# Counted places for the level runs, and float16 pairs for layer 1's mixer, in a two-layer hybrid attention block

## The chip, the cores and the metric

One NeuronCore of a Trainium2 chip runs the whole program. The metric is the device time of one execution in microseconds. The kernel is written by hand against the engines: TensorE (PE, with its weight loads as PEld), VectorE (DVE), ScalarE (ACT), GpSimd (POOL), and SyncE (SP), which issues nearly all DMAs. A scheduler places the instructions of each engine in one fixed order when the program is built; on the chip each engine then works through its own list in that order.

## The reference

512 tokens, 1024 features, two layers, all float32. Each layer is `x += mixer(rmsnorm(x))` and then `x += swiglu(rmsnorm(x))`; a last rmsnorm follows.

```python
def hybrid_mixer(h, ...):
    (hq, hf, hi, hog, gq, gk, gv, glr, gog, nq_, nkc, ..., ngate, mgate) = split_cols(h @ w_in)
    o_hg = chunked_gated_linear_attention(silu(hq), -expm1(log_f), hi, log_f)      # HGRN, 4 heads of 128
    y_hg = head_rmsnorm(o_hg, ...) * silu(hog)
    o_gla = chunked_gated_linear_attention(gq * 64 ** -0.5, gk, gv, log_a)         # GLA, 4 heads of 64/128
    y_gla = head_rmsnorm(o_gla, ...) * silu(gog)
    y_nsa = nsa_attention(q, kc, vc, ks, vs, kw, vw, gates)                        # 8 heads of 64
    g = sigmoid(mgate).reshape(B, T, 3, 1024)
    m = g[:, :, 0] * (y_hg @ w_br_hg) + g[:, :, 1] * (y_gla @ w_br_gla) + g[:, :, 2] * (y_nsa @ w_br_nsa)
    return m @ w_out

def swiglu(h, w_gate, w_up, w_down):                                               # 1024 -> 2816 -> 1024
    return (silu(h @ w_gate) * (h @ w_up)) @ w_down
```

## The kernel before, in words

**Dense products.** All weights are read once, in pieces of 128 x 1024 float32 (512 KB). A product is exact to float32 by pairs: both operands are split into a high and a low part, and `mm3` (L267) issues three matmuls of 128x128 by 128x512 for each block: high by high, high by low, low by high. `mm3` also chains every dense block after the one before (`dense_last`), so the dense matmuls of the program have one fixed order, 3600 a layer; other matmuls may be placed between them.

Two kinds of pairs exist. In the mixers, `wout`, FFN-down and the first two FFN pieces the parts are float32r: `weights` (L165) loads a piece into `wraw` (two buffers, DMA issued by SP), ACT copies it to `whi` (L282), and DVE subtracts to `wlo` (L283). In the rest of the FFN's gate and up the parts are float16: `scaled` (L186) loads into `xg` (eight buffers), ACT takes the sum of squares (`squares`, L184), POOL sums it over the partitions, DVE makes a power of two from it (`power`), and `split_by` scales and splits (L207, L208). The moving side of those is made by `x16` (L218), which also takes the norm's factor `rb` in, so the result needs one scale `ginv` at eviction and not `rb`.

**The mixer's dense work.** Column pieces (`A`: `hq`, `hf`, `gk`, `gq`, `hog`, `gog`, `mgate`, 44 of them) have the features on the partitions and are evicted by `evac` on DVE (L534: PSUM times `rb`). Token pieces (`Bg`: `hi`, `gv`, `n1`, `n2`, four pieces each, and the three uneven pieces of `w3` in `small`) go through `dense_t` with the tokens on the partitions. The products of the branches (`wbr`) and `wout` follow. `fill` spreads the 24 `mgate` pieces and the branch products over the later heads and over NSA, where they stand between the attention's small matmuls. `norm` makes `xg` (float32r pairs of x times the gain) and `rb`, and the factors per token (`rs`) with eight one-column matmuls (L348).

**Heads and level runs.** `attend` (L399) does one HGRN head, or two GLA heads at a time: 12 calls in all, six a layer. Its intra-chunk scores are made in seven levels. For each level `gated` takes ACT (L430) and DVE (L431, L434, L436) one after the other, from the level before; the results lie in `ahl`, which has four buffers. After each second level (and after the seventh) PE does a *level run*: 24 small float16 matmuls (12 for the last; twice as many for two GLA heads) into a PSUM buffer `s` (three of them), from which DVE copies by mask (L458). So an `attend` has four level runs, the program 48. The third and fourth need `ahl` buffers that the first frees. After them come the state products (L473), the output `o` (L492) and `finish`. Where a level run stands among the dense matmuls was the scheduler's choice.

**Order around layer 0's FFN.** After 22 pairs of gate and up (`for f`, L727), FFN-down has eight output blocks of 66 matmuls (L743), then layer 1 begins with `norm`, `hq` and `hf` of head 0, of head 1, and `hi`.

## Time and profile before

| | |
|---|---|
| median of 3 runs | 1904.47 us (1903.38 to 1906.08) |
| profiled execution, its own time | 1905.07 us |
| its span, first to last instruction | 1903.3 us |
| mean granted TensorE clock | 0.998 |
| layer 0: mixer and `wout` / FFN | to about 600 / to about 955 us |
| layer 1: mixer and `wout` / FFN | to about 1539 / to the end |

Times in rows are microseconds from the span's start. A busy time of PE counts modelled ends: a 128x512 matmul is shown as some 0.38 to 0.40 us long while the next one starts after less than 0.23, so a stream of them shows PE as busy throughout, and the pace is read from the starts. "Idle before" counts only what lies past the modelled end of the instruction before.

### The profile page before, as it was taken

To read this page: it belongs to the slowest core of one execution; us is meant where nothing else is said; L and a number is where in the kernel's file an instruction comes from. 1 tells how busy PE (TensorE), PEld (TensorE's weight loads), DVE (VectorE), ACT (ScalarE), POOL (GpSimd) and SP (SyncE) were. 2 spreads that over 40 slices of the span, in tenths; PEclk is the share of its full clock that TensorE was granted. 3 is DMA by queue.
4 is the path that set the end of the run, shared out by engine and by line. 5 is a ranking of instruction groups with operands and counts; after the bars stand their busy time and mean duration, and the time that the engine had idled before them with its cause. 6 is when DMAs were issued, how large, how long until landed. Compare 5 with 4: busy or idle time off the path is not lost.

```text
span 1903.3 us, 27551 instructions
## 1 busy us (share of the span) xinstructions
PE 1872.6 (98%) x10642; PEld 1359.3 (71%) x10642; DVE 1186.4 (62%) x2242; ACT 1020.6 (54%) x1766; POOL 43.2 (2%) x100
## 2 busy tenths in 40 slices
PE   9999999999999999999999999999999999999998
PEld 7778777777788444468887787777778874444787
DVE  7677867689766534323367787767896774443233
ACT  6556655378745755322255566543886466553222
POOL 0000000000000000000000000000000000000000
PEclk9999999999999999999999999999999999999999
DMA  4222213248733533023332222132586344330222
GB/s 164 84 72 77 78 62 100 78 95 162 193 100 95 207 100 103 30 71 107 116 95 78 75 74 81 53 106 73 118 168 164 116 155 144 101 110 1 89 89 97
DMA packets 142467, 194.24 MB, mean 102 GB/s; under 512 B 91552, under 2 KB 94208, under 8 KB 142336
## 3 DMA queue, kind: packets, MB, share of 16 engines
q1 hardware_dynamic: 142048, 192.35, 34.6%
q8 instruction: 83, 1.36, 0.3%
q14 instruction: 48, 0.39, 0.1%
q10 hardware_dynamic: 288, 0.14, 0.0%
HBM read 167.29 MB, written 4.19 MB: 90 GB/s over the span
## 4 chain that ended last, share of the span: by engine, by line
PE 80%; DVE 9%; issue 6%; ACT 3%; DMA 1%; POOL 0%; DVEq 0%; SPq 0%; ACTq 0%; POOLq 0%
PE mmf L271 8%; PE mmf L270 8%; PE mmf L269 8%; PE mm L269 5%; PE mm L271 5%; PE mm L270 5%; PE mmmgate L269 4%; PE mmmgate L271 4%; PE mmmgate L270 4%; PE s L998 2%; DVE wlo L283 2%; PE o L492 2%; DVE at L458 2%; DVE ahl L431 1%; PE o L1047 1%
## 5 line engine op out<-in xcount | busy, mean ns | idle before, releaser
L282 ACT ACTIVATE whi<-wraw 128x1024 fp32r<-128x1024 f32 (+2 forms) x242 | 232.5, 961 | 334.0 <-PE mm L270 122.5
L283 DVE TENSOR_TENSOR wlo<-wraw,whi 128x1024 fp32r<-128x1024 f32 (+2 forms) x242 | 266.4, 1101 | 163.5 <-ACT whi L282 158.7
L269 PE MATMUL mmmgate<-xg,whi 128*128 128x512 f32 x384 | 153.4, 399 | 0.0
L271 PE MATMUL mmmgate<-xg,wlo 128*128 128x512 f32 x384 | 151.5, 395 | 0.2
L270 PE MATMUL mmmgate<-xg,whi 128*128 128x512 f32 x384 | 151.3, 394 | 0.0
L208 DVE SCALAR_TENSOR_TENSOR whi<-xg,gsc,whi 128x1024 f16<-128x1024 f32 x38 | 48.8, 1284 | 138.0 <-ACT whi L207 138.0
L430 ACT ACTIVATE ahl<-kq 128x512 f16<-128x512 f32 x84 | 55.1, 656 | 79.1 <-DVE kq L434 66.2
L184 ACT ACTIVATE v<-xg 128x1024 bf16<-128x1024 f32 x76 | 79.9, 1051 | 26.8 <-DMA xg<-w 26.1
L207 ACT ACTIVATE wlo<-xg,gsc 128x1024 f16<-128x1024 f32 x38 | 43.6, 1147 | 78.2 <-PE mmf L271 78.2
L271 PEld LDWEIGHTS mmmgate<-xg,wlo 128*128 128x128 f32 x384 | 72.2, 188 | 15.3 <-DVE wlo L283 1.1
L269 PEld LDWEIGHTS mmmgate<-xg,whi 128*128 128x128 f32 x384 | 72.3, 188 | 14.3
L270 PEld LDWEIGHTS mmmgate<-xg,whi 128*128 128x128 f32 x384 | 72.3, 188 | 12.9
L739 DVE SCALAR_TENSOR_TENSOR ld<-mmf,ginv,ld 128x512 f32<-128x512 f32 x40 | 30.0, 750 | 73.5 <-PE mmf L271 73.5
L130 ACT ACTIVATE ld<-s,nm 128x128 f32<-128x128 f32 (+3 forms) x128 | 65.8, 517 | 15.4 <-DVE nm L1017 12.1
L271 PE MATMUL mmn<-whi,xg 128*128 128x512 f32 (+1 forms) x192 | 70.4, 367 | 0.0
L269 PE MATMUL mmn<-whi,xg 128*128 128x512 f32 (+1 forms) x192 | 70.2, 366 | 0.0
L1027 DVE SCALAR_TENSOR_TENSOR ahl<-ld,sums,ahl 128x128 f16<-128x128 f32 (+3 forms) x128 | 65.7, 547 | 6.7 <-ACT ahl L1026 5.9
L270 PE MATMUL mmn<-wlo,xg 128*128 128x512 f32 (+1 forms) x192 | 69.6, 362 | 0.0
L1026 ACT ACTIVATE ahl<-ld,sums 128x128 f16<-128x128 f32 (+3 forms) x128 | 65.2, 552 | 4.5 <-DVE sums L1023 1.8
L130 ACT ACTIVATE ld<-mmf,ginv 128x512 f32<-128x512 f32 x40 | 27.4, 684 | 73.8 <-PE mmf L271 73.8
L431 DVE TENSOR_TENSOR ahl<-kq,ahl 128x512 f16<-128x512 f32 x84 | 59.0, 702 | 7.1 <-ACT ahl L430 7.0
L1017 DVE TENSOR_REDUCE nm<-s 128x1 f32<-128x384 f32 (+3 forms) x96 | 56.3, 592 | 5.6 <-PE s L998 5.2
(474 smaller groups left out, 4982.7 us busy)
## 6 DMA issues: line engine op xcount, KB each, us to landing
wraw<-w SPq DMA_DIRECT2D x188, 512.0 KB, 3.5
xg<-w SPq DMA_DIRECT2D x76, 512.0 KB, 3.5
wraw<-w SPq DMA_DIRECT2D x57, 256.0 KB, 2.6
xt<-xT SPq DMA_DIRECT2D x16, 256.0 KB, 5.8
lr<-cw SPq DMA_DIRECT2D x16, 256.0 KB, 5.8
xd<-xt SPq DMA_DIRECT2D x8, 256.0 KB, 3.1
xt<-xd SPq DMA_DIRECT2D x8, 256.0 KB, 5.6
wraw<-w SPq DMA_DIRECT2D x4, 444.0 KB, 3.2
```

The costliest lines, as they stand in the source:

```text
L130: i = self.nc.scalar.activation(out, in_, func, **kw)
L184: self.nc.scalar.activation(self.st("v1", list(x.shape), BF), x, AF.Square, scale=scale, accum_out=ss)
L269: first = mm(out, a[0], b[0], start=start, stop=False)
L270: mm(out, a[0], b[1], start=False, stop=False)
L271: last = mm(out, a[1], b[0], start=False, stop=stop)
L282: nc.scalar.activation(hi, x, AF.Copy)
L283: nc.vector.tensor_tensor(lo, x, hi.bitcast(F32), op=ALU.subtract)
L430: nc.scalar.activation(hi, kq, AF.Copy)
L431: nc.vector.tensor_tensor(lo, kq, hi, op=ALU.subtract)
L1017: nc.vector.tensor_reduce(nm, pv, axis=AX.XY, op=ALU.max, negate=True)
L1026: nc.scalar.activation(ahl[:, 0, b], a[:, b], AF.Copy, scale=sums[:, b:b + 1])
L1027: nc.vector.scalar_tensor_tensor(ahl[:, 1, b], a[:, b], sums[:, b:b + 1], ahl[:, 0, b], op0=ALU.mult, op1=ALU.subtract)
```

## The change

**Level runs.** Each level run's first matmul is noted in `runs`, and each `mm3` notes its three matmuls in `passes`. At the end of the build an order is added for those of the 48 with a number in `LEVELS_AT`: the run comes after that many dense matmuls. It waits for no semaphore; it fixes the order on PE. In the program before, the runs of layer 0 stood after (in the order of the list, 0 marking the same free ones) 216, 216, 234, 240; 384, 384, 405, 411; 552, 552, 581, 590; 720, 720, 751, 761; 912, 912, 929, 930; 1056, 1056, 1075, 1094 dense matmuls, and those of layer 1 within a few of the same plus 3600.

**Layer 1 in float16 pairs.** All of layer 1's `A` and `Bg` pieces and `w3`, but for `hq` and `hf` of heads 0 and 1, are split to float16 by a scale (`pieces16`), with the moving side from `x16`, held in eight `y` buffers; one piece lies in one `whi` or `wlo` buffer in turn, and not in one of each. The sums of squares come from `presums`: 59 further loads of these pieces into `xg` during layer 0's FFN, each with an ACT Square, one or two after each gate/up pair from the fourth on (28), then up to five after each FFN-down block (31). Layer 1 then loads the pieces again as before.

**With it.** `evac16` on DVE multiplies by the piece's scale in place of `rb`; for `mgate` it also clamps, so `gate`'s own clamp (L767) falls away in layer 1. Layer 1's per-token factors fall away. The gates `m` of layer 1's first branch lie in `xg`.

```diff
+LEVELS_AT = (0, 0, 240, 246, 0, 0, 414, 420, 0, 0, 588, 597, 726, 726, 756, 768, 0, 921, 942, 948, 0, 1068, 1086, 1104, 0, 0, 3843, 3849, 0, 0, 4020, 4026, 0, 0, 4194, 4206, 0, 4347, 4374, 4380, 0, 4521, 4545, 4551, 0, 4668, 4689, 4710)
...
+    def presums(self, l):
+        nc, io = self.nc, self.io
+        w = lambda n, i: (io["w"][l, PIECES[n] + i], D)
+        ones = [(n, i) for n in ("hq", "hf") for i in range(2, 4)]
+        ones += [(n, i) for n, c in A_TILES[2:] for i in range(c)]
+        fours = ("hi", "gv", "n1", "n2")
+        srcs = [w(*k) for k in ones] + [w(n, i) for n in fours for i in range(4)]
+        srcs += [(io["w3"][l, :, a:b], b - a) for a, b in CUTS3]
+        self.pre = {k: i for i, k in enumerate(ones + list(fours) + ["w3"])}
+        sums = self.st("misc", [P, len(srcs)])
+        for j, (src, n) in enumerate(srcs):
+            raw = self.st("xg", [P, n])
+            nc.sync.dma_start(raw, src)
+            self.squares(sums[:, j:j + 1], raw)
+            if j < len(srcs) - 1:
+                yield
...
+        self.pexp, self.pscale = self.power(g, "misc", "pexp", "pscale")
+
+    def pieces16(self, key, srcs):
+        at = self.pre[key]
+        out = []
+        with self.hp():
+            for src, n in srcs:
+                raw = self.st("wraw", [P, n])
+                self.nc.sync.dma_start(raw, src)
+                self.turn = 1 - self.turn
+                t = self.st(("whi", "wlo")[self.turn], [P, 2, n], F16)
+                self.split_by(t[:, 0], t[:, 1], raw, self.pscale[:, at:at + 1])
+                out.append((t[:, 0], t[:, 1], self.pinv[:, at:at + 1]))
+        return out
...
@@ mm3
         self.dense_last = last.ins
+        self.passes += [first.ins, None, last.ins]
...
@@ attend
                             if last is not None:
                                 self.after(ins, last)
+                            elif m == j == 0 and ps is pss[0]:
+                                self.runs.append(ins)
...
+    def evac16(self, tag, ps, inv, scale, floor):
+        t = self.st(tag, [P, T]) if isinstance(tag, str) else tag
+        with self.hp():
+            if scale is not None:
+                self.nc.vector.tensor_scalar(t, ps, inv, scale, op0=ALU.mult, op1=ALU.mult)
+            elif floor is not None:
+                self.nc.vector.tensor_scalar(t, ps, inv, floor, op0=ALU.mult, op1=ALU.max)
+            else:
+                self.nc.vector.tensor_scalar(t, ps, inv, None, op0=ALU.mult)
+        return t
...
@@ layer
-        xg, rb, rs = self.norm(x, sp["g1"], True, l == 0)
+        xg, rb, rs = self.norm(x, sp["g1"], not self.pre, l == 0)
+        if self.pre:
+            xh = self.x16(x, sp["g1"], rb, [self.st("y", [P, 2, T], F16) for _ in range(KD)])
+            self.pinv = self.st("pinv", [P, len(self.pre)])
+            nc.vector.tensor_scalar(self.pinv.bitcast(I32), self.pexp, self.xoff, None, op0=ALU.add)
...
+        def A(name, n, tag, scale=None, floor=None):
+            if (name, n) in self.pre:
+                w = self.pieces16((name, n), [(io["w"][l, PIECES[name] + n], D)])
+                ps, = self.pair16(w, xh, f"{name}{n}")
+                return self.evac16(tag, ps, w[0][2], scale, floor)
...
+        def T3(name, srcs, width):
+            if name in self.pre:
+                w = self.pieces16(name, srcs)
+                return self.dense_t(w, xh, width, name), [w[0][2]] * NT
...
+        more = self.presums(l + 1) if l + 1 < DEPTH else iter(())
         acts = self.act_slots()
         for f in range(NF):
...
             self.split(*acts[f], t1)
+            for _ in range(int(1.5 * f) - int(1.5 * (f - 1)) if f >= 3 else 0):
+                next(more, None)
         s = Stream(self, l, PIECES["down"])
         last = l == DEPTH - 1
         for n in range(KD - last):
...
+            for _ in range(5):
+                next(more, None)
...
     def mgate(self, A, br, d, tag):
-        g = A("mgate", br * KD + d, tag)
+        g = A("mgate", br * KD + d, tag, floor=-44.0)
         with self.hp():
-            self.gate(g)
+            self.gate(g, floor=False)
         return g
...
@@ build
+        for run, at in zip(k.runs, LEVELS_AT):
+            if at:
+                k.after(run, k.passes[at - 1].name)
```

## Rows read from the trace of the kernel before

**Rows 1.** The page's busy time: engine, us, share of the span, instructions.

```profile
PE 1872.6 (98%) x10642; PEld 1359.3 (71%) x10642; DVE 1186.4 (62%) x2242; ACT 1020.6 (54%) x1766; POOL 43.2 (2%) x100
```

**Rows 2.** Stretches: length; busy (count) PE, PEld, DVE, ACT, POOL; clock; DMA; GB/s.

```profile
958.00:1003.00 45.00, 44.96 (x198) 36.83 (x198) 27.29 (x42) 23.59 (x39) 1.69 (x2) 1.00 0.30 91
1003.00:1340.00 337.00, 327.98 (x2124) 260.69 (x2123) 255.88 (x514) 178.64 (x300) 9.36 (x21) 1.00 0.24 77
1340.00:1447.00 107.00, 106.52 (x847) 84.88 (x846) 96.37 (x253) 94.42 (x242) 0.00 (x0) 1.00 0.77 151
615.00:650.00 35.00, 34.55 (x160) 17.75 (x159) 22.64 (x43) 30.91 (x51) 3.67 (x7) 1.00 0.70 252
650.00:740.00 90.00, 90.00 (x419) 40.79 (x418) 38.93 (x63) 50.11 (x71) 3.58 (x9) 1.00 0.32 100
850.00:940.00 90.00, 90.00 (x390) 73.06 (x389) 31.59 (x34) 24.25 (x28) 0.00 (x0) 1.00 0.34 112
```

**Rows 3.** PE in time order, layer 1 `gv`: start, length, line, tiles, shape.

```profile
1069.94 0.40 PE L269 MATMUL mmgv<-whi,xg 128*128 128x512 f32 x1
...
1081.99 0.39 PE L271 MATMUL mmgv<-whi,xg 128*128 128x512 f32 x1
```

**Rows 4.** PE in time order, layer 0's FFN, float16.

```profile
700.02 0.38 PE L270 MATMUL mmf<-ahl,wlo 128*128 128x512 f16 x1
...
707.79 0.38 PE L270 MATMUL mmf<-lr,whi 128*128 128x512 f16 x1
```

**Rows 5.** Groups by line, the level runs: busy us, mean ns, idle before, releaser.

```profile
L452 PE MATMUL s<-ahl 128*128 128x64 f16 x672 | 24.1, 193 | 6.2 <-DVE ahl L431 6.2
L452 PE MATMUL s<-ahl 64*128 64x64 f16 x672 | 15.1, 190 | 9.3 <-DVE at L458 6.5 <-DVE ahl L431 2.8
```

**Rows 6.** Who waited for whom: us in total, times, longest.

```profile
PE s L452 <- DVE ahl L431: 9.0, 17, 1.1
```

**Rows 7.** PE in time order, layer 0, HGRN head 0, later level runs.

```profile
64.94 0.39 PE L271 MATMUL mmn<-whi,xg 128*128 128x512 f32 x1
65.95 0.86 PE L452 MATMUL s<-ahl 128*128 128x64 f16 x24 [0.61 <-DVE ahl L431]
...
68.13 0.51 PE L452 MATMUL s<-ahl 128*128 128x64 f16 x12
```

**Rows 8.** PE in time order, layer 0, GLA pair 0, first level runs.

```profile
247.30 1.24 PE L452 MATMUL s<-ahl 64*128 64x64 f16 x60
...
251.52 0.88 PE L452 MATMUL s<-ahl 64*128 64x64 f16 x36 [1.39 <-DVE at L458]
```

**Rows 9.** Layer 1 NSA stretch, instructions on tile `mmmgate` alone: PE, PEld, DVE.

```profile
1340.00:1447.00 107.00, 57.28 (x218) 39.46 (x216) 6.38 (x10) 1.00 0.77 151
```

**Rows 10.** Groups by line on DVE, columns as in 5.

```profile
L283 DVE TENSOR_TENSOR wlo<-wraw,whi 128x1024 fp32r<-128x1024 f32 x184 | 224.8, 1222 | 140.8 <-ACT whi L282 140.0 <-DMA lr<-cw 0.3
L208 DVE SCALAR_TENSOR_TENSOR whi<-xg,gsc,whi 128x1024 f16<-128x1024 f32 x38 | 48.8, 1284 | 138.0 <-ACT whi L207 138.0
L534 DVE TENSOR_TENSOR y<-mmmgate,rb 128x512 f32<-128x512 f32 x32 | 22.1, 690 | 41.0 <-PE mmmgate L271 40.9
L666 DVE TENSOR_SCALAR ld<-s,sp 128x512 f32<-128x512 f32 x4 | 3.0, 751 | 9.1 <-PE s L664 9.1
L767 DVE TENSOR_SCALAR y<-y 128x512 f32<-128x512 f32 x32 | 13.5, 421 | 0.3
```

**Rows 11.** Groups by line on ACT.

```profile
L282 ACT ACTIVATE whi<-wraw 128x1024 fp32r<-128x1024 f32 x184 | 194.7, 1058 | 283.1 <-PE mm L270 122.5 <-issue 58.2 <-PE mmmgate L270 37.0
L184 ACT ACTIVATE v<-xg 128x1024 bf16<-128x1024 f32 x76 | 79.9, 1051 | 26.8 <-DMA xg<-w 26.1
L207 ACT ACTIVATE whi<-xg,gsc 128x1024 f16<-128x1024 f32 x38 | 43.2, 1136 | 0.5 <-DVE gsc L180 0.5
```

**Rows 12.** PE in time order, layer 1's first norm.

```profile
956.23 0.95 PE L348 MATMUL s<-ones,og 128*128 128x1 f32 x8
```

**Rows 13.** The page's DMA issues: count, KB each, median us from issue to landing.

```profile
xg<-w SPq DMA_DIRECT2D x76, 512.0 KB, 3.5
```

89 lines of the change are left out of this document (54 added, 35 removed).

## The prediction

> **What bounds the kernel now.** I read the page's busy times first. TensorE is busy 98% of the span [rows 1], its granted clock 1.00 in every stretch I use [rows 2], so a microsecond counts only if it leaves TensorE's stream. The table of stretches says where it has company: in layer 1's heads DVE is busy 256 of 337 us, in its NSA stretch 96 of 107 with ACT at 94, while in the FFN's gate and up (650 to 740) and down (850 to 940) PE has no idle time at all and DVE is at 43% and 35% [rows 2]. A busy time with modelled ends hides the pace, so third I read PE's starts in order of time: 53 steps of float32r take 12.05 us, 227.4 ns each [rows 3]; 36 steps of float16 with the same 512 columns take 7.77 us, 215.8 ns [rows 4]. Fourth, what makes PE stand still: of the 1903.3 us of span PE is idle in 31 [rows 1], and the groups by line put 6.2 and 9.3 of these ahead of the level runs [rows 5]. The waits name the makers: 17 times the DVE subtraction that makes `ahl` [rows 6], and, in GLA, the mask copies that give back the PSUM buffer [rows 5, 8].
>
> So there are two removable things: some 20 us of standing still, half in each layer, and 11.6 ns in every converted matmul.
>
> **Part 1, the level runs.** An example: the matmul ahead starts at 64.94, the run at 65.95 [rows 7]. A dense neighbour would have started 0.23 us later, so 0.78 us are lost, of which the row shows 0.61 as idle; 0.16 us (0.39 us of modelled length less 0.23) is hidden in each such stall. With 17 stalls on `ahl` [rows 6] and 4 on the PSUM buffer (one in each GLA call; the program has two calls a layer), the total is 15.5 [rows 5] + 21 x 0.16 = 18.9 us.
>
> The new places take this away where the delay covers the chain. In HGRN head 0 the third run goes from 234 to 240 dense matmuls: 6 x 0.227 = 1.36 us against 0.78, and the fourth again 6 behind: 0.69 + 1.36 = 2.05 us after the third, against 2.18 before [rows 7], with 0.58 us in hand. Of the others that stalled, most are put 5 to 18 matmuls later, 1.1 us and more, so they are covered as well. In layer 1 six float16 matmuls are 1.29 us, and the same head's places (27 matmuls after the first runs, where layer 0 has 24) make up for that.
>
> GLA's second run is another case. Its later part waits for the mask copies and starts at 251.52; the first run starts at 247.30 and takes 0.7 us [rows 8]. Put 9 dense matmuls on, it comes at 248.0 + 2.05 = 250.1 and still meets copies that DVE does not reach earlier; its first 12 matmuls (60 less 48 in the row) need none of them and take 0.3. I leave 1.1 us in each of the four: -4.4. Part 1: 18.9 - 4.4 = **14.5 us** (bounds: 18.9 if DVE's order shifts in its favour; 0 if each delay comes out again behind the run). For the second bound: queued behind a late run on PE are the state products and `o` of its head, on DVE its mask copies. A head's turn is 168 dense matmuls (the places 216 to 384), 38 us, which for most of that time need none of this head's results, so 1.4 us later is not late. I take the upper half for that reason. Nothing else moves: the order waits for no semaphore, and no DMA and no other queue belongs to it.
>
> **Part 2, float16 in layer 1's mixer.** Converted are 40 column pieces of 24 matmuls and 16 token pieces of 24: 960 + 384 = 1344, each 227.4 - 215.8 = 11.6 ns shorter [rows 3, 4]: 15.6 us. The 96 of 296 columns in `w3` are not in the rows at float16; between nothing and the same saving in proportion, 96 x 6.7 ns = 0.6 us, I take 0.6. In NSA, 218 of the matmuls [rows 9] stand between attention steps where DVE is 90% busy and ACT 88% [rows 2]. If these set the pace there, 218 x 11.6 ns = 2.5 us don't arrive; I take off a third, 0.8. Part 2: **15.4 us** (bounds 13.1 to 17, the upper one with the contended steps at 0.229 us in place of 0.227).
>
> Both paces hold across stages: 90 us of gate and up hold 419 matmuls, 90 us of FFN-down in float32r 390 [rows 2]. The Trainium skill, "TensorE: Matmul & The Clock Gate", section "Back-to-back issue gap", gives the spacing as columns over 2.4 GHz plus 2.5 ns, 215.8 ns for 512, and names no data type there. The float16 rows agree to the digit; by that rule alone the conversion would be worth nothing, but the trace has 227.4 for float32r.
>
> What part 2 costs beside it:
> - DVE. Splitting a piece takes 1284 ns in place of 1222, ACT's half 1136 in place of 1058 [rows 10, 11]: 56 pieces, 3.5 and 4.4 us. An eviction that multiplies by a column from a per-partition scalar takes 751 ns (L666, also out of PSUM) against 690 [rows 10]: 40 x 0.06 = +2.4. Each `mgate` loses its clamp: 24 x 0.42 = -10.1. `x16` adds 8 x (0.75 + 0.69) = 11.5 us on DVE and some 5 on ACT. In the heads DVE goes from 256 of 337 to some 254 of 320, which hides it; in NSA it falls with PE. I cost it at nothing.
> - The added wait. The first float16 piece, `hi`, waits for `rb` and `x16`, and behind it stands the whole dense chain. Ahead of it are 96 float32r matmuls, 21.8 us, and its four pieces want two of the eight parts every 5.2 us. DVE has 27.3 of 45 us busy there [rows 2]; 11.5 more make 38.8. It fits; if DVE took the head's own chain first, the wait would cost some 5 us. The level chain of head 0 also comes later, but its first runs stand 120 matmuls behind `hi`'s start.
> - The per-token factors: eight matmuls of 0.95 us together drop out of PE's stream [rows 12]: **-0.8 us**.
>
> **Part 3, the sums of squares.** 59 loads of 512 KB on SP, 59 Squares of 1.05 us and an accumulator read on ACT, one POOL sum. In gate and up, ACT is busy 50.1 of 90 us [rows 2]; 1.5 Squares per pair of 10.4 us add 18%. The eight `xg` buffers then serve 3.5 loads a pair and still hold two pairs. In FFN-down, ACT is busy 24 of 90 us; up to five per block of 66 x 0.231 = 15.2 us add 41%. The DMA goes there from 112 GB/s to as much as 112 + 5 x 0.524 MB / 15.2 us = 284. The fastest stretch shown has 252 GB/s at a DMA share of 0.70, and PE lost 0.45 us of 35 in it [rows 2]. Cost: I take **+1.0 us**, twice that row, with 0 and 7 as ends (one late piece of 1 us at each of seven blocks; a gain is excluded, since nothing leaves this stage). The cover is the two raw and two split buffers of a stream that wants a piece every 24 x 0.23 = 5.6 us; what happens without it is the last rival.
>
> **The sum.** 1905.1 (profiled) - 14.5 - 15.4 - 0.8 + 1.0 = 1875.4. The median of the runs lies 0.6 under the profiled execution: **1875**, 1.5% faster.
>
> **The rivals.**
> - Stalls that move. The level runs come later, and so do their mask copies, state products and `o`; if PE then waits at those for what it no longer waits before, part 1 is worth nothing: 1905.1 - 15.4 - 0.8 + 1.0 - 0.6 = 1889. For it: the third run starts just when DVE lets it [rows 7], so this chain is a serial one, ACT to DVE to ACT. Against it: it is serial over 24 to 36 of a head's 168 dense matmuls.
> - The mixer's pace is DVE's and ACT's. Then part 2 gives nothing: 1890. For it: 90% in NSA [rows 2]; against it: 76% in the heads [rows 2], where most of the converted matmuls are.
> - One pace for both types: if the 11.6 ns belong to the busy mixer around the matmul and not to its type, they stay, and part 2 gives nothing: 1890 again. Against it: FFN-down is float32r and quiet, and still holds 390 where gate and up hold 419 [rows 2]. The Trainium skill's page named above has a rule that would come out here, one gap whatever the type.
> - Everything arrives: GLA's PSUM wait goes too, the contended steps count, and DVE's relief by the clamps shortens other chains: 1905.1 - 18.9 - 17 - 0.8 - 0.6 = 1868, with a few us more for the last point: 1862 to 1868.
> - Slower: sums of squares ahead of the weights. SP issues in order and the eight free `xg` buffers let it issue up to eight loads ahead of FFN-down's next piece. At 252 GB/s a load takes 2.1 us, so the piece lands 8 x 2.1 + 3.5 [rows 13] = 20 us after its issue. Two raw and two split buffers cover about 2 x 5.6 - 2.3 (splitting) = 9 us. PE would stand 11 us at each of seven blocks, +77 us: 1950. With five loads ahead it is 14 us against 9, +35 us: 1909. It decides from about five loads in a row, and an ACT that meets a Square whose load has not landed adds to it, since the next weights' split queues behind. Against it: nothing forces the loads to come in bursts, since each waits for a buffer that a Square gives back; and at 0.70 DMA share the trace shows no such stall. Milder forms end between 1885 and 1905.
> The Trainium skill, "DMA: Bandwidth & Descriptors", section "Queues, rings and completion order", says that on each DMA engine the descriptors of a ring are consumed in order; no row here shows two such loads overtaking or not, and by it the burst would cost what this rival says.
>
> **How the numbers follow.** Chances: forecast (1868 to 1883) 0.58; moved stalls 0.14; DVE's pace 0.07; one gap 0.02; everything arrives 0.11; sums of squares ahead of the weights 0.08, of which 0.06 end slower and 0.02 about level. About 0.2% is what a measurement of this kernel can tell from no change. Faster 0.92, same 0.02, slower 0.06. The range 1861 to 1891 takes in the bounds of all three parts and the cases about 1890; outside lie the slow rival and the last of the best case. Likeliest sign and likeliest time agree, so one range does.
>
> **What would show it.** Right: idle time ahead of L452 falls from 15.5 us to some 4, all of it in the GLA form; starts of `hog`, `gv` and `mgate` in layer 1 are 0.216 us apart; layer 1's mixer and `wout` are shorter by some 23 us, layer 0's mixer by some 7, and layer 0's FFN is as long as before. Wrong: idle time at L473, L492 or L998 that was not there (moved stalls); DVE over 95% in a stretch of layer 1 with PE waiting for `wlo`, `whi` or `s` (its pace); gaps in PE at FFN-down's first matmul of a piece, with ACT's split waiting for a DMA (loads ahead); a gap at the first `hi` matmul (`x16`).

## The result, and the profile after

The changed kernel takes **1891.9 us** (median of 6 runs, 1891.0 to 1892.9) against 1905.8 (median of 6 of the kernel before): a ratio of 0.993 [0.9917, 0.9943]. It is 13.9 us faster, where 30 were forecast, and lies just above the range. The profiled execution took 1891.8 us, 1890.0 of them span.

The busy times of the page, beside [rows 1]: TensorE has 17 us less, and is still at 98%; ACT has 67 us more.

```profile
PE 1855.3 (98%) x10634; PEld 1234.1 (65%) x10634; DVE 1193.3 (63%) x2244; ACT 1088.0 (58%) x1892; POOL 47.0 (2%) x102
```

**The pace came.** Layer 1's `gv` in order of time (start, length, line, tiles, shape), to be set beside [rows 3]:

```profile
1063.60 0.38 PE L309 MATMUL mmgv<-wlo,y 128*128 128x512 f16 x1
...
1069.42 0.38 PE L309 MATMUL mmgv<-whi,y 128*128 128x512 f16 x1
```

27 steps in 5.82 us are 215.6 ns each, where float32r had 227.4. The Trainium skill, "TensorE: Matmul & The Clock Gate", section "Back-to-back issue gap", has a formula that gives 215.8 ns for 512 columns and names no data type. The float16 rows agree, the float32r rows differ, and the measurement decides.

**The sums of squares cost nothing.** Stretches of layer 0's FFN (columns as in [rows 2]). The first two lines are gate and up and FFN-down of the kernel after; the third and fourth are the stretch with the most loads, after and before.

```profile
646.00:736.00 90.00, 90.00 (x419) 40.79 (x418) 38.56 (x63) 69.66 (x110) 4.41 (x11) 1.00 0.61 199
846.00:936.00 90.00, 90.00 (x391) 73.05 (x390) 31.23 (x34) 24.25 (x28) 0.00 (x0) 1.00 0.35 111
790.00:846.00 56.00, 56.00 (x255) 32.72 (x253) 19.85 (x32) 45.85 (x79) 1.15 (x3) 1.00 0.75 271
```
```profile
794.00:850.00 56.00, 56.00 (x255) 32.83 (x254) 18.50 (x22) 16.88 (x22) 0.00 (x0) 1.00 0.15 45
```

With 271 GB/s in place of 45, and ACT busy 46 of 56 us in place of 17, TensorE starts the same 255 matmuls in 56 us.

**The level runs are better, the state products worse.** Groups by line and shape (L491 is L452 of before, L514 is L473), then TensorE's waits (us, times, longest):

```profile
L491 PE MATMUL s<-ahl 128*128 128x64 f16 x672 | 24.0, 193 | 3.1 <-DVE ahl L470 3.1
L491 PE MATMUL s<-ahl 64*128 64x64 f16 x672 | 14.0, 190 | 7.6 <-DVE at L499 6.1 <-DVE ahl L470 1.5
L514 PE MATMUL s<-kq 128*128 128x256 f32 x32 | 10.1, 399 | 5.9 <-DVE kq L483 4.3 <-DVE kq L482 1.6
```
```profile
PE s L491 <- DVE at L499: 6.1, 6, 1.6
PE s L491 <- DVE ahl L470: 4.6, 8, 1.1
PE s L514 <- DVE kq L483: 4.3, 4, 1.5
PE s L514 <- DVE kq L482: 2.8, 3, 1.2
```

Idle time ahead of the runs fell from 15.5 us [rows 5] to 10.7, waits on `ahl` from 17 to 8 [rows 6]. But the state products, which had 1.1 us before, have 7.4 (5.9 of them in the heads' form, shown above; the rest stands in GLA's).

One head shows how. Layer 0, head 0, TensorE and then DVE after the change, and, before it, TensorE's state product and the DVE instruction that finished its operand:

```profile
66.93 0.87 PE L491 MATMUL s<-ahl 128*128 128x64 f16 x24
...
69.11 0.53 PE L491 MATMUL s<-ahl 128*128 128x64 f16 x12
...
71.64 1.55 PE L514 MATMUL s<-kq 128*128 128x256 f32 x8 [0.77 <-DVE kq L483]
```
```profile
68.40 0.69 DVE L473 TENSOR_TENSOR kq<-kq,fl 128x512 f32<-128x512 f32 x1
69.01 1.22 DVE L322 TENSOR_TENSOR wlo<-wraw,whi 128x1024 fp32r<-128x1024 f32 x1
70.15 0.43 DVE L499 COPY_PREDICATED at<-lm,s 128x256 f32<-128x256 uint8 x1
...
70.69 0.43 DVE L499 COPY_PREDICATED at<-lm,s 128x256 f32<-128x256 uint8 x1
...
71.22 0.28 DVE L483 TENSOR_SCALAR kq<-kq,fl 128x128 f32<-128x128 f32 x1
```
```profile
71.31 1.55 PE L473 MATMUL s<-kq 128*128 128x256 f32 x8
```
```profile
70.88 0.28 DVE L443 TENSOR_SCALAR kq<-kq,fl 128x128 f32<-128x128 f32 x1
```

The run at 65.95 [rows 7] had lost 0.61 us; now the runs stand at 66.93 and 69.11 and lose nothing. The state product is ordered by nothing in the change and stands behind 251 dense matmuls in both kernels. Its operand `kq` is ready when DVE has finished the level chain, a weight split (1.22 us) and two mask copies that are queued between: at 71.50. In the kernel before, the lost 0.6 us had made the state product late enough, and `kq` was ready at 71.16, since the earlier runs had let DVE make their mask copies sooner. Now the state product is 0.6 us earlier and `kq` 0.34 later, and TensorE waits 0.77 (and 0.16 more under the modelled end of the matmul ahead).

**Where it went by stage.** The start of the same dense matmul, counted from the first, in the kernel before and in four others; the columns are how much longer (+) or shorter each stage is than before, in us, in one profile each. A fall of TensorE's clock, 1.7 us, stands in some of the GLA entries (last section).

| stage (dense matmuls) | after | level runs alone | float16 alone | all places moved |
|---|---|---|---|---|
| layer 0, HGRN heads (to 912) | +1.2 | +1.0 | 0.0 | -3.6 |
| layer 0, GLA to `wout` (to 2016) | -4.5 | -3.8 | -1.6 | -4.4 |
| layer 0, FFN (to 3600) | -0.2 | -0.3 | +0.3 | 0.0 |
| layer 1, norm and first pieces (to 3816) | -2.6 | 0.0 | -2.6 | -2.6 |
| layer 1, HGRN heads (to 4512) | -5.3 | -1.7 | -2.7 | -12.2 |
| layer 1, GLA (to 4800) | -2.0 | -4.2 | -0.9 | -3.9 |
| layer 1, NSA (to 5424) | 0.0 | +0.7 | -1.0 | +0.9 |
| the rest | +0.2 | 0.0 | +0.3 | +0.2 |
| sum | -13.2 | -8.3 | -8.1 | -25.5 |

Two things want a cause: HGRN heads in which the cleared runs bring little (and in layer 0 nothing), and an NSA in which shorter matmuls bring nothing.

### The profile page after: what moved, and what is told of

It is laid out like the page before. It is cut to its first block, busy times and chain, and to the rows that moved or that the text cites. A ratio compares the mean times of both kernels' runs of the same rounds, so it can differ in the third digit from the quotient of the medians.

```text
span 1890.0 us, 27814 instructions
## 1 busy us (share of the span) xinstructions
PE 1855.3 (98%) x10634; PEld 1234.1 (65%) x10634; DVE 1193.3 (63%) x2244; ACT 1088.0 (58%) x1892; POOL 47.0 (2%) x102
## 4 chain that ended last, share of the span: by engine, by line
PE 80%; DVE 13%; ACT 3%; issue 2%; DMA 2%; POOL 0%; DVEq 0%; SPq 0%; ACTq 0%; POOLq 0%
PE mmf L309 8%; PE mmf L308 8%; PE mmf L307 8%; PE mm L309 6%; PE mm L307 6%; PE mm L308 6%; PE mmmgate L309 4%; PE mmmgate L307 4%; PE mmmgate L308 4%; PE s L1084 2%; DVE at L499 2%; PE o L533 2%; DVE ahl L470 2%; DVE kq L473 1%; PE o L1133 1%
## 5 line engine op out<-in xcount | busy, mean ns | idle before, releaser
L321 ACT ACTIVATE whi<-wraw 128x1024 fp32r<-128x1024 f32 (+2 forms) x183 | 170.5, 932 | 275.8 <-PE mm L308 112.4
L322 DVE TENSOR_TENSOR wlo<-wraw,whi 128x1024 fp32r<-128x1024 f32 (+2 forms) x183 | 194.9, 1065 | 138.0 <-ACT whi L321 134.1
L189 ACT ACTIVATE v<-xg 128x1024 bf16<-128x1024 f32 (+1 forms) x135 | 141.3, 1047 | 37.2 <-DMA xg<-w 35.4
L307 PEld LDWEIGHTS <-wlo 128*128 128x128 f16 x488 | 47.8, 98 | 56.7 <-issue 2.5
L309 PEld LDWEIGHTS <-wlo 128*128 128x128 f16 x488 | 47.8, 98 | 56.6 <-issue 0.6
L308 PEld LDWEIGHTS <-wlo 128*128 128x128 f16 x488 | 47.8, 98 | 55.4 <-issue 0.4
L307 PEld LDWEIGHTS <-whi 128*128 128x128 f16 x472 | 46.1, 98 | 56.8 <-issue 3.6
L309 PEld LDWEIGHTS <-whi 128*128 128x128 f16 x472 | 46.2, 98 | 54.7 <-DVE whi L249 1.1
L308 PEld LDWEIGHTS <-whi 128*128 128x128 f16 x472 | 46.2, 98 | 53.3 <-issue 0.4
L307 PE MATMUL mmmgate<-xg,whi 128*128 128x512 f32 x192 | 76.5, 398 | 0.0
L309 PE MATMUL mmmgate<-xg,wlo 128*128 128x512 f32 x192 | 75.8, 395 | 0.1
L308 PE MATMUL mmmgate<-xg,whi 128*128 128x512 f32 x192 | 75.5, 393 | 0.0
L1084 PE MATMUL s<-lv,xt 128*128 128x512 f32 (+2 forms) x192 | 59.4, 392 | 2.9 <-ACT ld L135 2.4
```

The lines of the kernel that those rows point to most:

```text
L189: self.nc.scalar.activation(self.st("v1", list(x.shape), BF), x, AF.Square, scale=scale, accum_out=ss)
L307: first = mm(out, a[0], b[0], start=start, stop=False)
L308: mm(out, a[0], b[1], start=False, stop=False)
L309: last = mm(out, a[1], b[0], start=False, stop=stop)
L321: nc.scalar.activation(hi, x, AF.Copy)
L322: nc.vector.tensor_tensor(lo, x, hi.bitcast(F32), op=ALU.subtract)
```

## Experiments on the heads

**Level runs alone.** The kernel before with the numbers and their order, and nothing else of the change.

```diff
+LEVELS_AT = (0, 0, 240, 246, ... 4668, 4689, 4710)
...
+        for run, at in zip(k.runs, LEVELS_AT):
+            if at:
+                k.after(run, k.passes[at - 1].name)
```

> The kernel before with the counted places of the level runs alone (all 48 numbers of the change; no float16 in the mixer, no sums of squares ahead). Theory A (stalls moved): in the HGRN heads the idle time leaves the level runs (L452's 128-row form) and comes back at the head's state products, whose place is not ordered and whose operands come from the same chain on DVE; only GLA gains, some 3.6 us a layer as layer 0 showed. Time 1898 to 1900 us, ratio 0.996 to 0.9975; idle ahead of the level runs 10 to 11 us, ahead of the state products 6 to 8 us. Theory B (the prediction: a later run is not late, and what ate the gain is the float16 part): 14.5 us less, 1891 us, ratio 0.9925; idle ahead of the state products stays at 1 us.

Measured: 1896.8 us, 0.9952 [0.9939, 0.9966], 9.1 us less, between the two. By group:

```profile
L455 PE MATMUL s<-ahl 128*128 128x64 f16 x672 | 24.1, 193 | 0.2 <-DVE ahl L434 0.2
L455 PE MATMUL s<-ahl 64*128 64x64 f16 x672 | 14.0, 190 | 4.8 <-DVE at L463 4.4 <-DVE ahl L434 0.4
L478 PE MATMUL s<-kq 64*128 64x128 f32 (+3 forms) x128 | 21.9, 344 | 5.9 <-DVE kq L447 3.0 <-DVE kq L446 1.7 <-DVE at L463 0.8
```

The idle time ahead of the runs is 5.0 us, nearly all in the GLA form, which is what the prediction named; theory A had 10 to 11, which is what the runs keep once the float16 part is there too. Of the 6.0 us taken from the heads' form, 4.8 stand at the state products now (1.1 to 5.9). And not all of the gain is waits: 1.7 us of this kernel's -3.8 in layer 0's GLA are a fall of TensorE's clock that the kernel before has there and this one hasn't (last section).

**Float16 alone.**

```diff
-LEVELS_AT = (0, 0, 240, 246, ...)
+LEVELS_AT = (0,) * 48
```

> The changed kernel without the counted places (all 48 numbers zero): float16 pairs in layer 1's mixer and the sums of squares in layer 0's FFN. Theory A: the shorter matmuls give 21.6 us of dense pace, of which attention in NSA keeps some 6.7 and layer 1's heads and GLA some 5 as new waits, so 8 to 10 us arrive: 1896 to 1898 us, ratio 0.995 to 0.996. Theory B (the prediction's part 2, 15.4 us, arrives in full and only the level runs failed): 1890 us, ratio 0.992. Layer 0 is as long as before by both.

Measured: 1899.3 us, 0.9966 [0.9954, 0.9979], 6.5 us less.

```profile
L491 PE MATMUL s<-ahl 128*128 128x64 f16 x672 | 24.0, 192 | 10.2 <-DVE ahl L470 10.1
L491 PE MATMUL s<-ahl 64*128 64x64 f16 x672 | 15.1, 190 | 10.0 <-DVE at L499 6.9 <-DVE ahl L470 3.1
```

20.2 us idle ahead of the runs, against 15.5 [rows 5]. The dense matmuls are shorter, so a run that stands behind a given number of them comes sooner, and the chain on ACT and DVE has not become faster: 4.7 us of what float16 gains became waits here. (The -1.6 us of this kernel in layer 0's GLA, which float16 doesn't touch, are again the clock's fall in the kernel before.) The two parts alone add up to 15.6 us, the change gave 13.9.

**The state products ordered too.** The first state product of each HGRN head is noted and put after a number of dense matmuls, some 10 behind its place.

```diff
+STATES_AT = (261, 432, 618, 780, 0, 0, 3864, 4038, 4230, 4398, 0, 0)
...
+                    else:
+                        self.firsts.append(ins)
...
-        for run, at in zip(k.runs, LEVELS_AT):
+        for run, at in list(zip(k.runs, LEVELS_AT)) + list(zip(k.firsts, STATES_AT)):
```

> The changed kernel with one order more: the first state product of each HGRN head is put after a counted number of dense matmuls too, some 10 behind where it stood (261 for 251, 432 for 422, 618 for 605, 780 for 768; 3864 for 3852 and so on in layer 1; GLA's stay free). Theory A (the wait at the state products is only a matter of their place): the 5.9 us of idle time ahead of them go, and 1.4 us more that the modelled length hides; 1885 us, ratio to the kernel before 0.989. Rival C (the chain behind is late as well): the wait goes on to the output product or to the next head's first products; 1890 to 1892 us, ratio 0.992 to 0.993, with idle time at L533 grown by what L514 lost.

Measured: 1887.6 us, 0.9905 [0.9891, 0.9918]; 4.3 less than the changed kernel, between the two theories. Head 0 in order of time, and the groups:

```profile
73.02 1.48 PE L515 MATMUL s<-kq 128*128 128x256 f32 x8
```
```profile
L492 PE MATMUL s<-ahl 128*128 128x64 f16 x672 | 24.1, 193 | 5.8 <-DVE ahl L471 5.0 <-ACT y L322 0.8
L515 PE MATMUL s<-kq 128*128 128x128 f32 (+3 forms) x128 | 22.4, 361 | 1.5 <-DVE kq L483 1.2
```

The state product no longer waits (7.4 to 1.5), and nothing appears at the output product (0.6 us of idle time before, 0.1 now). But 2.7 us come back at the level runs (3.1 to 5.8). I take it that each head that is sooner brings the next head's chain nearer; the next run tests that by moving the later heads alone.

**Places of heads 2 and 3 once more.** Level runs and state products, beside those of the run before (the numbers that change):

```diff
-588, 597, 726, 726, 756, 768    4194, 4206, 0, 4347, 4374, 4380
+594, 603, 726, 750, 774, 780    4203, 4218, 4326, 4356, 4386, 4393
-STATES_AT = (261, 432, 618, 780, 0, 0, 3864, 4038, 4230, 4398, 0, 0)
+STATES_AT = (261, 432, 621, 792, 0, 0, 3864, 4038, 4239, 4410, 0, 0)
```

> The changed kernel with the state products ordered as in the run before (10 dense matmuls later) and with the places of those level runs moved once more that still stalled there: heads 2 and 3 of both layers, 6 to 18 dense matmuls later (594, 603; 750, 774, 780; 4203, 4218; 4326, 4356, 4386, 4393), and their state products 3 to 12 behind (621, 792, 4239, 4410). Theory A (each wait is a matter of where the counted place stands against the chain on ACT and DVE): of the 6.6 us that still wait on ahl some 5 go: 1882 to 1883 us, ratio to the kernel before 0.988. Rival C (a later run makes the rest of the chain later by as much): 1887 to 1888 us as with the state products alone, the idle time turning up at the state products, the outputs or the next head's first products.

Measured: 1881.9 us, 0.9866 [0.9849, 0.9882], as theory A has it.

```profile
L492 PE MATMUL s<-ahl 128*128 128x64 f16 x672 | 24.2, 193 | 0.4 <-DVE ahl L471 0.4
```

The heads' runs wait 0.4 us in all, the state products 1.4.

**GLA's places.** The four calls:

```diff
-921, 942, 948   1068, 1086, 1104   4521, 4545, 4551   4668, 4689, 4710
+930, 951, 957   1077, 1095, 1107   4530, 4554, 4560   4677, 4701, 4713
```

> As the run with the heads' places, and GLA's level runs 3 to 9 dense matmuls later as well (930, 951, 957; 1077, 1095, 1107; 4530, 4554, 4560; 4677, 4701, 4713). The changed kernel still idles 6.1 us there for the mask copies that give back the PSUM buffer. If the place decides, 3 to 5 us of these go: 1878 to 1880 us, ratio 0.986. If DVE comes to the copies later as well (they are queued behind other work, the prediction's reason for leaving 1.1 us in each call), the 6.1 us stay and the time is that of the heads' places alone.

Measured: 1881.6 us, 0.9868 [0.9853, 0.9882], no more than before it, though the GLA form's idle time fell from 7.7 to 3.8 us. Layer 1's first call was 1.9 us longer in the profile. With that call back:

```diff
-4530, 4554, 4560
+4521, 4545, 4551
```

> As the run with the heads' places, with GLA's level runs 3 to 9 dense matmuls later in three of the four calls; layer 1's first GLA call, which lost 1.9 us to its later places, keeps the change's places (4521, 4545, 4551). Theory A (places against the chain): the gains of the single calls add, 1879.5 to 1881 us, ratio to the kernel before 0.986. Rival C: 1882 us and more, since what GLA gains comes back at its state products.

Measured: **1879.3 us**, 0.9854 [0.9842, 0.9867], 12.5 us faster than the changed kernel, with the same instructions. The reason given for the last step doesn't hold as given, though: in the profile of the run before, that call wasn't longer by its waits, but because TensorE's granted clock had fallen in it.

```profile
1185.00:1190.00 5.00, 5.00 (x19) 2.65 (x18) 1.16 (x2) 2.54 (x8) 0.00 (x0) 0.50 0.15 52
1190.00:1195.00 5.00, 5.00 (x18) 2.59 (x17) 3.13 (x5) 3.33 (x7) 0.84 (x2) 0.81 0.00 0
```

Mean clocks of 0.50 and 0.81 in two stretches of 5 us lose 3.4 us, more than the 1.9. It wasn't that one profile: the four executions of that kernel have mean clocks of 0.995 to 0.997, the four of this one 0.998 to 0.999. So the lower clock came with that order of instructions; what in the order brings it about isn't shown. The last column of the table, "all places moved", is this kernel: layer 1's heads give back 12.2 us.

```profile
L492 PE MATMUL s<-ahl 64*128 64x64 f16 x672 | 13.5, 190 | 5.5 <-DVE at L500 5.5
```

## Experiments on NSA

The NSA stretch here is from the first score product to the last value product of layer 1. The first line of each group below gives them for the changed kernel (ns shortest, median, longest; first and last start):

```profile
L1084 PE MATMUL s<-lv,xt x96: 276/397/582, 1327.0 to 1424.2; 128*128 128x512 f32 x48, 128*128 128x384 f32 x32, 128*128 128x256 f32 x16
...
L1133 PE MATMUL o<-v,lr x480: 192/193/204, 1342.1 to 1448.5; 128*128 128x64 f16 x160
```

The stretch before and after, columns as in [rows 2]:

```profile
1342.60:1461.30 118.70, 118.25 (x988) 94.88 (x986) 101.67 (x262) 101.23 (x251) 0.00 (x0) 1.00 0.81 167
```
```profile
1327.00:1448.50 121.50, 117.81 (x991) 71.41 (x990) 99.41 (x251) 102.39 (x251) 0.00 (x0) 1.00 0.78 163
```

It became 2.8 us longer. Counted by TensorE's starts, the time from a dense matmul to the next instruction fell (75.6 us for 318, then 72.9 for 322), and the same after score products rose from 24.1 to 26.9 and after value products from 14.0 to 16.6. What was gained to either side of the stretch (53.7 to 51.6 us ahead of it, 33.0 to 32.4 behind) is spent in it.

**Less of TensorE.** For 16 `mgate` pieces the high-by-low matmul is left out.

```diff
-                self.mm3(p, (hi[:, c], lo[:, c]), xh[k], k == 0, k == KD - 1)
+                self.mm3(p, (hi[:, c], lo[:, c]), xh[k], k == 0, k == KD - 1, label.startswith("mgate") and int(label[5:]) >= KD)
...
-        mm(out, a[0], b[1], start=False, stop=False)
+        if not two:
+            mm(out, a[0], b[1], start=False, stop=False)
```

> The changed kernel without the high-by-low matmul of the mgate pieces of branches 1 and 2 in layer 1 (16 pieces, 128 dense matmuls less; that term of the product is left out). They stand in and around layer 1's NSA. Theory A (DVE and ACT set NSA's pace): where the matmuls stand inside the stretch from the first to the last score product its length stays at 96 to 97 us (within 2 us), and TensorE's busy time there falls well below 95%. Rival D (TensorE sets the pace there): the stretch is 0.216 us shorter for every matmul left out in it, 12 us and more. The whole time is 1892 less 128 x 0.216 = 27.6 us by D, 1864; by A only what lies outside the stretch comes through, 1875 to 1885.

Measured: 1886.0 us, 0.9895 [0.9881, 0.9908]: 5.9 of 27.6 us arrive. The stretch is 112.9 us with 136 dense matmuls (29 us) less in it, and TensorE waits 15.7 us at the score products for ACT to give back their PSUM buffer. Of the 112.9 us, 3.4 are falls of the clock (mean 0.97).

```profile
1332.50:1445.40 112.90, 93.74 (x856) 60.08 (x855) 95.24 (x243) 97.57 (x243) 0.00 (x0) 0.97 0.75 155
```
```profile
PE s L1085 <- ACT ld L135: 15.7, 17, 4.2
```

So less work on TensorE shrinks the stretch to some 110 us, and there something else holds it.

**Less of DVE, of ACT, of the transposes.** Each alone:

```diff
+                if l:
+                    nc.gpsimd.memset(ahl[:, 1, b], 0.0)
+                else:
...
```

> The changed kernel with the low part of layer 1's attention weights (L1113 on DVE, 59 instructions and 29.6 us of the 97.5 us between NSA's first and last score product) replaced by a memset to zero on GpSimd: that term of the attention's output is left out. TensorE's and ACT's instructions stay as they are. If DVE sets the pace of that stretch, it shrinks by well over 5 us, until TensorE (93.8 busy, some 4 us of it removable) or ACT (86 us busy) is next: 90 to 93 us, and the whole time 1885 to 1888 us. If ACT or the round trip through ACT sets it, the stretch stays within 2 us of 97.5 and the whole time at 1890 to 1892 us.

```diff
+        if not (self.pre and br):
             with self.hp():
                 self.gate(g, floor=False)
```

> The changed kernel without the three ACT functions of layer 1's mgate gates of branches 1 and 2 (Exp, Ln, Exp: their sigmoid is left out). Between NSA's first and last score product these are 18 of ACT's instructions and 11.8 of its 86 us. If ACT sets the pace there, the stretch shrinks by 5 us and more (from 97.5 us) and the whole time comes to 1884 to 1887 us; if DVE alone does, it stays within 2 us and the whole time at 1890 to 1892 us. If both this run and the one without DVE's low parts shrink, the softmax as a whole (a unit's steps in turn on DVE and ACT) is the pace and not one engine.

```diff
-            ins = nc.sync.dma_start(aT.rearrange("p t (j c) -> p (t j) c", c=P), u["ahl"].rearrange("p t c -> p (t c)"), transpose=True)
+            n = 1 if l else 2
+            ins = nc.sync.dma_start(aT[:, 0:n].rearrange("p t (j c) -> p (t j) c", c=P), u["ahl"][:, 0:n].rearrange("p t c -> p (t c)"), transpose=True)
...
-                        ins = mm(Os[i][:, h], aT[:, t, b * nb + j * P:b * nb + (j + 1) * P],
+                        ins = mm(Os[i][:, h], aT[:, 0 if l else t, b * nb + j * P:b * nb + (j + 1) * P],
```

> The changed kernel with half of each DMA transpose in layer 1's attention: only the high part of the weights is turned, and the product of the low part reads the high part again. TensorE, DVE and ACT do what they did. Rival E (the transposes set NSA's pace): SP's issue of each (1.23 us) and its landing (3.3 us) get shorter, and the whole time falls to 1884 to 1887 us. Theory A2 (the round trip through the PSUM buffers of the scores): within 2 us of 1892 us.

Measured: 1893.0 us (0.9928 [0.9913, 0.9943]), 1895.0 (0.9937 [0.9922, 0.9952]) and 1890.6 (0.9919 [0.9904, 0.9934]). The stretches, in that order:

```profile
1327.70:1449.60 121.90, 117.95 (x991) 71.84 (x990) 73.89 (x187) 102.93 (x251) 21.03 (x56) 1.00 0.79 163
```
```profile
1328.40:1452.00 123.60, 117.61 (x994) 72.24 (x993) 98.96 (x250) 84.28 (x216) 0.00 (x0) 1.00 0.77 161
```
```profile
1328.40:1447.40 119.00, 117.67 (x993) 71.42 (x992) 99.49 (x251) 102.32 (x251) 0.00 (x0) 1.00 0.48 123
```

26 us off DVE and 18 us off ACT bring nothing. Halving the transposes brings 2.5 us in the stretch: the time after value products is back at 14.0 us. So the part of the loss that stands at the value products comes from late transposes (the longest wait for one is 1.6 us in the changed kernel). The part at the score products doesn't: the time after them is 26.8 us with half transposes, against 26.9.

**The round trip of the scores.** Without the row maximum in layer 1, and, in both layers, with the two heads' score products one after the other:

```diff
-            nc.vector.tensor_reduce(nm, pv, axis=AX.XY, op=ALU.max, negate=True)
+            if not l:
+                nc.vector.tensor_reduce(nm, pv, axis=AX.XY, op=ALU.max, negate=True)
...
-                         bias=nm[:, b:b + 1], accum_out=sums[:, b:b + 1])
+                         bias=0.0 if l else nm[:, b:b + 1], accum_out=sums[:, b:b + 1])
```

> The changed kernel without the row maximum in layer 1's attention (L1103 on DVE, 46 instructions of 0.59 us between the first and the last score product; the exponential takes the scores as they are). This takes one link out of the round trip PE score -> DVE maximum -> ACT exponential -> free PSUM buffer -> next PE score, of which three buffers `s` allow one and a half pairs ahead. Theory A2 (that round trip sets NSA's pace, since removing other DVE and ACT work changed nothing): TensorE no longer waits at the score products for ACT, layer 1's NSA gives back most of the 6.7 us of waits that the shorter matmuls turned into, and the whole time comes to 1884 to 1887 us. Rival E (the DMA transposes of the weights, DMA share 0.77 in the stretch, set it): the time stays at 1890 to 1893 us and the waits stand at the value products.

```diff
-            for u in (ub, ua):
-                step(u["ps"], u["q"], kh, start=True, stop=False)
-            for u in (ua, ub):
-                step(u["ps"], u["q"], kl, start=False, stop=False)
             for u in (ua, ub):
+                step(u["ps"], u["q"], kh, start=True, stop=False)
+                step(u["ps"], u["q"], kl, start=False, stop=False)
                 for b in range(n):
...
```

> The changed kernel with the score products of an NSA pair in another order, in both layers: first all products of the first head (high, low, mask), then all of the second, where before the two heads' products alternate. Nothing is left out, and the mixer's order ahead of NSA is the same. The first head's scores are then ready some 0.5 us sooner for DVE and ACT, and the second's PSUM buffer is wanted later. Theory A2 (the round trip PE score -> DVE -> ACT -> free PSUM buffer is what TensorE waits for at the score products): these waits shrink in both layers, 2 to 6 us less than the changed kernel's 1891.9: 1886 to 1890 us. Rival F (the queues run in lock-step on something else): 1890 to 1894 us.

Measured: 1901.9 us (0.9978 [0.9969, 0.9988]), slower than the changed kernel against both theories, and 1890.9 (0.993 [0.9908, 0.9953]), no change. The first has a stretch of 132.6 us; three times in it the clock falls (last section), which is some 5 of the 11 us, and where the rest comes from isn't settled: with an instruction gone, the scheduler may have ordered other engines' lists anew, too. Neither run supports the round trip as the one limit.

**The order of the scores.** Each of the 24 score pairs is put where it stood before, counted in dense matmuls. On the changed kernel, then on the best one, then half-way on the best one:

```diff
+SCORES_AT = (4962, 4962, 4975, ... 5203, 5205)
...
+                if l and u is ub:
+                    self.pairs.append(ins)
...
+        for ins, at in zip(k.pairs, SCORES_AT):
+            k.after(ins, k.passes[at - 1].name)
```

> The changed kernel with the first score product of each of layer 1's 24 NSA pairs ordered after as many dense matmuls as it stood behind in the kernel before (4962 to 5205; in the changed kernel they stand up to 30 earlier, 4958 to 5182). Nothing is left out. Theory G (the part of the float16 gain that NSA loses is a matter of order: the rebuilt order puts the scores, counted in dense matmuls, ahead of what ACT and the transposes can serve, and TensorE waits there): the stretch from the first score to the last value product, 118.7 us before and 121.5 us after, falls to 116 to 118 us, and the whole time to 1886 to 1889 us. Rival D2 (DVE, ACT and DMA as a whole can't serve NSA faster, wherever the scores stand): the stretch stays at 121 us and more and the time at 1891 to 1893 us, the waits standing at other products.

> The best of the runs on places (heads, and GLA in three of four calls; 1879.3 us) with the same order of the score products. Theory G: 1873 to 1877 us, ratio to the kernel before 0.983. Rival D2: 1879 us.

> As the run before, with each score pair half-way between its place in the kernel before and its place in the changed one. Theory G with a bound between: 1874 to 1878 us. Rival D2: 1879 us.

Measured: 1889.5 us (0.991 [0.9893, 0.9926]), 1878.8 (0.9857 [0.9842, 0.9872]) and **1877.7** (0.9847 [0.9832, 0.9862]). The intervals overlap those without the order (0.993, 0.9854): about 2 us at best. The stretch is 121.6 us with the old places, of which 1.7 are a fall of the clock (0.66 in one stretch of 5 us), and 119.8 with the half-way ones, where it has none. On the best kernel without the order it is 122.4. The order thus explains 1.7 to 2.6 us of the stretch's length, and not that shorter matmuls don't make it shorter.

**All three off at once.** Half transposes and no gate functions, as above, and no low part on DVE; then the same with the matmuls left out of TensorE's run as well.

```diff
+                if not l:
+                    nc.vector.scalar_tensor_tensor(ahl[:, 1, b], a[:, b], sums[:, b:b + 1], ahl[:, 0, b],
...
```

> The changed kernel with three loads of layer 1's attention stretch taken off together, where each alone moved little: no low part of the weights on DVE (L1113), half of each transpose (the value product reads the high part in its place), and no ACT functions in the mgate gates of branches 1 and 2. TensorE's matmuls are the same. If DVE, ACT and DMA together held TensorE back by the 5 us of waits seen there, the stretch from the first score to the last value product (121.5 us) falls to the 116 us that TensorE's own steps take, and the time to 1885 to 1887 us. If the waits are TensorE's own in-order round trip, the stretch stays at 119 us and more, 1889 us and more.

> As the run before, and also without the high-by-low matmul of the 16 mgate pieces (128 dense matmuls less, as in the run on TensorE's work alone, where the stretch took 112.9 us and 5.9 of 27.6 us arrived). If DVE, ACT and DMA together were what that run ran into, the stretch falls by another 10 us and more, to 103 us or less, and most of the 27.6 us arrive: 1863 to 1868 us. If not, the stretch stays at 110 to 113 us: 1878 to 1884 us.

Measured: 1892.7 us (0.9931 [0.9915, 0.9948]) and 1870.0 (0.9811 [0.9797, 0.9826]).

```profile
1325.30:1448.90 123.60, 119.00 (x993) 72.47 (x990) 73.15 (x186) 82.95 (x216) 0.00 (x0) 0.99 0.48 119
```
```profile
1332.60:1428.30 95.70, 88.81 (x855) 56.53 (x853) 65.36 (x178) 80.15 (x213) 0.00 (x0) 1.00 0.57 129
```

Less of TensorE alone made the stretch 109.5 us (112.9 less the clock's 3.4), less of the others, alone or all three, leaves it at 119 to 124, both together make it 95.7. There are two limits: TensorE's own stream, which with its waits takes about 120 us, and the softmax with its transposes at about 110. This shows why a large relief of TensorE alone arrives only in part. It doesn't explain why the small one of this change didn't arrive, since the stretch still stands well above the second limit.

**What holds TensorE at the score products.** The time from a score product to the next start is 24.1 us in the two kernels whose layer 1 mixer is float32r (before, and level runs alone). It is 26.8 to 27.7 in all ten with float16 in which the stretch has no fall of the clock and all of TensorE's matmuls, whatever else was taken off or moved; with all three off, and one fall of the clock, it is 27.6. The profile shows next to no idle time behind these products (0.1 us at most). So it goes with the type of the dense matmuls around them. A float32 matmul that stands behind a 16-bit one takes some 0.1 us longer to the next start (rows in the last section). Before, 30 float32 matmuls of the stretch stood so; after the change it is 49, since the scores stayed float32 and the `mgate` matmuls around them became float16. An estimate from the starts of both kernels: what these matmuls take beyond the same shape behind a float32 one went from 2.3 to 5.2 us, and 1.1 us of that come back, since some start sooner behind the float16 matmul. Of the 2.6 us that shorter matmuls save in this stretch, the change of type thus takes back 1.7; late transposes take 2.5 (half transposes gave them back), and waits at the score products for ACT grew from 0.4 to 1.5 us. Less the 2.6 us saved, these come to 2.7, about the 2.8 us by which the stretch grew. No run here took the type changes away by themselves.

## Why the prediction was wrong, point by point

**What bounds the kernel** held: TensorE is busy 97 to 99% of the span in every variant, and each microsecond gained came out of its stream.

**Part 1, the size of the waits** held: the prediction saw 18.9 us, left 4.4 in GLA, and said that the idle time ahead of the runs falls to some 4, all in the GLA form; alone, it fell to 5.0, 4.8 of them there. **Part 1, the second bound failed.** "A head's turn is 168 dense matmuls ... so 1.4 us later is not late." Most of those 168 need nothing of the head, but its state product stands 5 matmuls behind the last run (11 before), and this place was not moved. It was read as queued behind the run on TensorE; what it waits for is the same chain on DVE, a few instructions further on, and the run's mask copies, which now come ahead of it there. "Nothing else moves" left that out. The rival of moved stalls named the right mechanism and L473 as the sign; it got 0.14, and its argument "this chain is a serial one" was the one to follow. Part 1 measured 9.1 us alone, not 14.5, nearly all of it in GLA, and some 1.7 of it the clock's. The rival's own sum, part 1 worth nothing, is out as well; that 1891.9 lies near its 1889 is chance, since part 2 fell short too.

**Part 2, the pace** held to the digit (215.6 ns against 215.8). **Part 2's costs at nothing failed**, in two terms. In the heads DVE's busy share was taken as cover ("to some 254 of 320, which hides it"). A share says nothing of a chain: runs and state products stand behind a number of dense matmuls, and come sooner when these are shorter; float16 alone added 4.7 us of waits at the runs. In NSA "I take off a third, 0.8" took too little: the stretch became 2.8 us longer, and took back what the dense matmuls to either side had gained. TensorE's own price for a float32 product behind a float16 one, some 1.7 us there, is in no term of the sum, and late transposes and waits for ACT took the rest. Part 2 brought 6.5 us alone, not 15.4. The signs by stage say the same: layer 0's mixer is some 3.4 us shorter where some 7 were named, layer 1's some 9.9 where it was some 23.

**The per-token factors** held (the norm's stretch is 0.9 us shorter), **the first float16 piece** did not wait for `x16` (its first matmul starts 0.22 us behind the last of `hf`), and **part 3** cost 0 where +1.0 was taken (layer 0's FFN is 0.2 us shorter). The rival of loads ahead of the weights did not occur at 271 GB/s.

**One pace for both types** is out by the rows of `gv`. **The mixer's pace is DVE's and ACT's**, said at 90% in NSA, is at most half right: with their transposes they hold NSA at some 110 us, which the change didn't come down to, and they don't set the heads' pace, where places alone gave the time back.

With the state products, the places of the later heads and of GLA moved too, and in the second also the scores', the same two parts give 27 to 28 us (1879.3 and 1877.7 us) of the 30 forecast. That isn't the sum come true: those kernels have orders that the forecast one hasn't, and NSA's stage gives next to nothing in them (0.9 us longer and 1.2 shorter than before). The range missed by 1 us because the moved stalls and the loss in NSA came together, and each had been counted only as a case by itself.

## What to carry to other kernels

When a stall is the end of a serial chain on other engines, look for the next instruction that reads that chain and move its place together with the one that stalls; the stall will otherwise be found there. Places counted in instructions of a stream come sooner when the stream gets faster, so set them again after each such change. In a stretch in which three engines are near 90%, look for a second limit below the first, and count a relief of one engine only down to it. And when some of the matmuls in a mixed stream change their type, count the places where a float32 one then follows a 16-bit one.

## What the runs showed of the hardware

TensorE's clock falls for a moment in these dense stages, though its mean is 0.998. In stretches of 5 us, kernel before and kernel after, both in GLA:

```profile
300.00:305.00 5.00, 3.63 (x43) 3.02 (x44) 4.53 (x11) 1.52 (x4) 0.00 (x0) 0.75 0.35 105
305.00:310.00 5.00, 5.00 (x65) 3.83 (x65) 4.62 (x9) 2.39 (x3) 0.00 (x0) 0.91 0.24 67
```
```profile
1190.00:1195.00 5.00, 3.40 (x81) 2.01 (x80) 4.41 (x12) 2.14 (x4) 0.00 (x0) 0.96 0.18 56
1195.00:1200.00 5.00, 5.00 (x21) 3.21 (x21) 1.30 (x3) 1.98 (x6) 0.31 (x1) 0.70 0.00 0
```

The two granted levels are 2.4 and 1.2 GHz, so 0.25 and 0.09, or 0.04 and 0.30, missing in 5 us are 1.7 us lost each time. Just ahead of each fall TensorE had stood in one wait, of 1.9 us in the kernel before and 1.6 in the kernel after, both at a level run of GLA. It doesn't always fall then. The same run in the best kernel (second line) waits as long, and its clock stays:

```profile
1193.97 0.52 PE L491 MATMUL s<-ahl 64*128 64x64 f16 x23 [1.60 <-DVE at L499]
```
```profile
1182.78 0.52 PE L492 MATMUL s<-ahl 64*128 64x64 f16 x23 [1.60 <-DVE at L500]
```

The run on level runs alone has no wait as long in its mixers, and no fall but the one at the program's end, which every kernel here has; the one without the row maximum has four beside that, three of them in NSA. A wait thus can cost 1.7 us more than it shows, and two kernels that differ by 2 us in a single profile may differ by nothing else. In the stage table, layer 0's GLA has the fall in the kernel before and with all places moved: 1.7 us of the other three entries (-4.5, -3.8, -1.6) are this fall's absence. Layer 1's GLA has it in the changed kernel and with float16 alone, which without it would stand at -3.7 and -2.6. Whole executions of one kernel differ by it, too: of the kernel before, beside the experiments, the five with a mean clock of 0.999 took 1903.7 us on average, the nine with 0.995 or 0.996 took 1907.8.

A float32 matmul takes longer to the next start when a 16-bit one stands ahead of it. Three score products of the changed kernel, behind a float16 and behind a float32r matmul:

```profile
1345.24 0.38 PE L307 MATMUL mmmgate<-y,whi 128*128 128x512 f16 x1
1345.45 0.97 PE L1084 MATMUL s<-lv,xt 128*128 128x512 f32 x3
1346.26 0.40 PE L1084 MATMUL s<-causal,ident_b 128*128 128x128 bf16 x4
...
1354.71 0.40 PE L309 MATMUL mmbr1d<-kq,wlo 128*128 128x512 f32 x1
1354.94 0.86 PE L1084 MATMUL s<-lv,xt 128*128 128x512 f32 x3
1355.65 0.40 PE L1084 MATMUL s<-causal,ident_b 128*128 128x128 bf16 x4
```

From the start of the three to the next it is 0.81 us in the first case, 0.71 in the second. In layer 1's NSA stretch, a score product of 512 columns takes a median of 338 ns to the next start behind a 16-bit instruction (19 of them, the shortest 318) and 235 behind a float32 one (29); in the kernel before it is 315 (3) and 236 (45). What makes the difference isn't shown.
